# The opening pair of feed-forward tiles with gate and up alternating, and half of the last output projection's low halves by an adding DMA

## The chip, the cores and the metric

The kernel runs on one core of a Trainium2 chip. The metric is the time of one execution in microseconds (us), as the device counts it; three runs of the kernel before are at hand, and one more execution that the hardware profiler recorded.

## The reference, cut to what matters

One layer for 1088 tokens (1024 of a new stream, 64 of a running one), width 1024. Only the parts that the change touches are written out:

```
xn   = rmsnorm(x, norm_mix);  proj = xn @ w_in          # then three recurrent mixers on slices of proj
mix  = concat(oA, oB, oC)                               # 1088 x 1024
x    = x + mix @ w_out                                  # output projection, 1024 x 1024
xn2  = rmsnorm(x, norm_ffn)
hid  = silu(xn2 @ w_gate) * (xn2 @ w_up)                # feed-forward, 22 column tiles of 128
x    = x + hid @ w_down
y    = rmsnorm(x, norm_final)
```

## The kernel before, in words

**Tiles.** Tokens stand along the free axis in three groups of 384, 384 and 320 (groups 0, 1, 2); the width stands on the 128 partitions in 8 blocks. Each float32 operand is split in two: a high half that ScalarE (ACT) rounds to the matmul's format (`whi` for weights, line 117 or 1359), and a low half, the value less its high half. A product is then three products: high by high, high weight by low operand, low weight by high operand. A low half of a weight (`wlo`) is made in one of two ways: VectorE (DVE) subtracts (line 122 or 1360), or ACT writes the negated high half (line 119) and a DMA that GpSimd (POOL) issues adds the weight to it from memory (line 120). `weights(src, False)` chooses the first, `weights(src)` the second.

**Stages.** Up to about 440 us lie the input projection and the mixers. The program opens with `uproj(2)`, two column tiles of the input projection for group 2; `part` (line 1142) loads their weights in four halves. Then come the output projections, `outproj(0)`, `outproj(1)` and `outproj(2)`, 8 column tiles `dm` each; `outproj(2)` lies at 535.7 to 566.7 us. It begins with dm 0 and 1 together and takes the others one by one. `finish_dm` (line 187) adds the result to x (line 189) and sums squares (lines 211, 214). For the feed-forward's norm, `row_sums` sums squares over the partitions on TensorE (PE), `inv_rms` makes 1/rms by some fifteen short DVE instructions that end in two diagonal tiles `dg` (line 243), and `spread` lets PE broadcast them; the product of x with it is line 1295 for groups 0 and 1. `keep` (line 1285) has POOL store x in memory.

**Feed-forward.** The two halves of the width and groups 0 and 1 form 2x2 blocks, and `quad` (line 1390) makes a pair of column tiles with 7 block products instead of 8 (Winograd's form). Its operands are sums and differences of blocks of x: b11, d1, b22, s, d2, r2, r1, each of 4 blocks of 128x384, made by `operand` (line 1299): a sum `xs` (line 1305), ACT's cast (line 1307), DVE's low half (line 1308). `xs`, and the copies `t` and `u` in `quad`, are temporaries from one ring of four buffers (tag `xT`). Of the weights' sums, `raw` and `sm`, line 1396 is the DVE instruction. `quad` runs b11, b22, s, d1, d2, r2, r1; b11's result is copied by ACT to `t` (line 1407) before d1 is added into the same accumulator. One `product` is 12 matmuls. Group 2 is done plainly (`plain`, line 1382), with operands x2h and x2l that `x2prep` makes (DVE lines 264 and 266, ACT 265). For the first pair of tiles the order is: gate's quad, row sums and spread of group 2, `x2prep(2)`, up's quad, four plain products.

**What sets the order.** PE's order is the order in which the code calls `mm` (line 76 chains them). For the other engines a scheduler sets a fixed order when the program is built; `first()`, `soon()` and `high_priority` move an instruction forward in it. On the chip each engine then takes its instructions in that order, and waits at the first that is not ready.

## Time and profile before

| | us |
|---|---|
| three runs: median (lowest, highest) | 1385.15 (1383.03, 1387.94) |
| the profiled execution | 1381.88 |
| its span, first to last instruction | 1380.1 |
| PE busy in it | 1275.0 (92%) |
| DVE, ACT, POOL busy | 913.5, 660.0, 224.2 |
| output projection of group 2 to the end of the opening pair: from, to | 535.73, 648.52 |

The three runs differ by 4.9 us. The profiled execution is 3.3 us under their median; of its time 1.8 us lie outside the span. Busy time is the sum of an engine's instructions; a matmul's end is modelled. "Idle before" an instruction names what ended the idle time. The granted clock is 1.00 when TensorE runs at 2.4 GHz and 0.50 at 1.2 GHz.

### The profile page before, as it was taken

The numbers are of one execution on the slowest core, as the hardware profiler recorded it, in microseconds if no ns is written. First come the engines' busy times: TensorE is split into PE (matmuls) and PEld (weight loads), VectorE is DVE, ScalarE is ACT, GpSimd is POOL, SyncE is SP. The second block draws the span as 40 slices with busy tenths as digits, with TensorE's granted clock in tenths as the row PEclk, the third lists the DMA queues.
The fourth block names the chain that finished last, engine by engine and source line by source line (L and its number), as shares of the span: only waits on it lengthen the run. The fifth ranks groups of instructions, "written<-read, shape, count | busy, mean of one in ns | idle before, by whom it ended". The sixth has DMA issues, their size and how long they took to land.

```text
span 1380.1 us, 21112 instructions
## 1 busy us (share of the span) xinstructions
PE 1275.0 (92%) x7608; PEld 1214.8 (88%) x7608; DVE 913.5 (66%) x2206; ACT 660.0 (48%) x1288; POOL 224.2 (16%) x278
## 2 busy tenths in 40 slices
PE   7987998989988999759999999999999999999995
PEld 7876897878777889659999999999999999999985
DVE  9875798857766668976475437543763476346687
ACT  7766657768885444434243224412442243133463
POOL 2334354424342000020100000010001000100000
PEclk8997999999998899779999999999999999999997
DMA  9977687768884346303812551254125412631543
GB/s 285 287 148 180 138 172 147 172 142 177 164 188 107 104 162 212 116 15 96 164 39 71 117 96 38 77 107 92 55 71 110 80 54 77 107 78 62 184 141 111
DMA packets 94330, 170.60 MB, mean 124 GB/s; under 512 B 11425, under 2 KB 31473, under 8 KB 94225
## 3 DMA queue, kind: packets, MB, share of 16 engines
q1 hardware_dynamic: 70080, 108.26, 25.9%
q0 software_dynamic: 24144, 60.99, 25.0%
q8 instruction: 60, 0.98, 0.3%
q14 instruction: 46, 0.37, 0.1%
HBM read 134.76 MB, written 33.86 MB: 122 GB/s over the span
## 4 chain that ended last, share of the span: by engine, by line
PE 51%; DVE 3%; DMA 1%; issue 1%; ACT 0%; DVEq 0%; ACTq 0%
PE q L76 51%; DMA res<-st 1%; DVE wlo L122 1%; DVE u L1429 0%; DVE dg L243 0%; DVE x1r L1353 0%; DVE hl L1452 0%; DVE u L1430 0%; DVE sil L1450 0%; ACT whi L1359 0%; DVE sacc L214 0%; DVE sc L150 0%; DVE sc L149 0%; DVE sc L148 0%; DVE x1r L1480 0%
## 5 line engine op out<-in xcount | busy, mean ns | idle before, releaser
L117 ACT CAST whi<-raw 128x512 fp32r<-128x512 f32 (+1 forms) x232 | 139.5, 607 | 101.0 <-PE q L76 40.9
L76 PE MATMUL mm<-xh,whi 128*128 128x384 f32 (+1 forms) x480 | 168.8, 360 | 17.9 <-ACT whi L117 9.9
L76 PE MATMUL q<-hl,whi 128*128 128x384 f32 (+1 forms) x528 | 173.2, 332 | 2.7 <-DVE hl L1452 2.7
L76 PE MATMUL q<-hh,whi 128*128 128x384 f32 (+1 forms) x528 | 172.9, 331 | 2.1 <-ACT hh L1451 1.7
L76 PE MATMUL mm<-xl,whi 128*128 128x384 f32 (+1 forms) x480 | 159.6, 340 | 4.5 <-DVE xl L332 4.5
L120 POOL DMA_DIRECT2D wlo<-in_w_in_dram x112 | 99.4, 971 | 211.9 <-ACT wlo L119 180.1
L1482 DVE COPY st<-q 128x384 f32<-128x384 f32 x80 | 41.4, 524 | 134.3 <-PE q L76 118.5
L1493 POOL DMA_DIRECT2D res<-st x40 | 34.0, 851 | 585.9 <-DVE st L1482 499.7
L76 PEld LDWEIGHTS mm<-xh,whi 128*128 128x128 f32 x480 | 95.3, 200 | 25.5 <-ACT whi L117 10.5
L76 PE MATMUL q<-hh,wlo 128*128 128x384 f32 (+1 forms) x528 | 111.7, 330 | 0.0
L1359 ACT CAST whi<-raw 128x512 fp32r<-128x512 f32 x128 | 78.1, 621 | 67.4 <-PE q L76 53.9
L1360 DVE TENSOR_TENSOR wlo<-raw,whi 128x512 fp32r<-128x512 f32 x128 | 87.5, 685 | 29.6 <-ACT whi L1359 14.2
L76 PEld LDWEIGHTS q<-hl,whi 128*128 128x128 f32 x528 | 100.3, 190 | 4.9 <-DVE hl L1452 4.9
L76 PE MATMUL q<-x2l,whi 128*128 128x320 f32 x352 | 103.8, 309 | 0.0
L76 PE MATMUL q<-x2h,whi 128*128 128x320 f32 x352 | 103.8, 309 | 0.0
L76 PEld LDWEIGHTS q<-hh,whi 128*128 128x128 f32 x528 | 100.1, 190 | 4.0 <-ACT hh L1451 3.6
L122 DVE TENSOR_TENSOR wlo<-raw,whi 128x512 fp32r<-128x512 f32 (+1 forms) x120 | 80.1, 672 | 34.3 <-ACT whi L117 29.4
L76 PEld LDWEIGHTS mm<-xl,whi 128*128 128x128 f32 x480 | 94.8, 198 | 9.0 <-DVE xl L332 6.0
L76 PE MATMUL mm<-xh,wlo 128*128 128x384 f32 (+1 forms) x480 | 93.4, 335 | 6.1 <-DMA wlo<-in_w_in_dram 6.0
L1396 DVE TENSOR_TENSOR sm<-raw 128x512 f32<-128x512 f32 x66 | 45.6, 691 | 75.0 <-DMA raw<-in_w_up_dram 57.3
L76 PEld LDWEIGHTS q<-hh,wlo 128*128 128x128 f32 x528 | 91.6, 190 | 0.0
L76 PEld LDWEIGHTS mm<-xh,wlo 128*128 128x128 f32 x480 | 82.5, 193 | 8.9 <-DMA wlo<-in_w_in_dram 8.7
(467 smaller groups left out, 2930.8 us busy)
## 6 DMA issues: line engine op xcount, KB each, us to landing
raw<-in_w_in_dram SPq DMA_DIRECT2D x112, 256.0 KB, 4.3
wlo<-in_w_in_dram POOLq DMA_DIRECT2D x112, 256.0 KB, 6.0
res<-st POOLq DMA_DIRECT2D x40, 544.0 KB, 6.0
raw<-in_w_down_dram SPq DMA_DIRECT2D x56, 256.0 KB, 2.7
raw<-in_w_out_dram SPq DMA_DIRECT2D x48, 256.0 KB, 3.1
raw<-in_w_gate_dram SPq DMA_DIRECT2D x48, 256.0 KB, 2.9
raw<-in_w_up_dram SPq DMA_DIRECT2D x48, 256.0 KB, 3.0
xg<-in_x_dram SPq DMA_DIRECT2D x8, 512.0 KB, 6.3
```

The lines of the kernel that those rows point to most:

```text
L76: in_order(PE.matmul(out, lhsT, rhs, start=start, stop=stop, **kw).ins)
L117: ins = A.copy(hi[:, :n, :], raw[:, :n, :]).ins
L120: G.dma_start(lo[:, :n, :], src[:, h0:h0 + n, :], accum_op=OP.add)
L122: tt(lo[:, :n, :], raw[:, :n, :], hi[:, :n, :].bitcast(F32), op=OP.subtract)
L1359: A.copy(hi, src)
L1360: tt(lo, src, hi.bitcast(F32), op=OP.subtract)
L1396: tt(t_, a, b, op=op)
L1482: (A.copy if gi == 1 else V.tensor_copy)(st[:, t0:t0 + T], o[:, :T])
L1493: nc.gpsimd.dma_start(res[:, dm, :], st, accum_op=OP.add)
```

## The change

Nine edits, in the order of the diff.

1. `outproj(2)`'s sum of squares stands in another buffer (tag `hh` instead of `sil`).
2. In `outproj(2)` the weights of the odd dm (1, 3, 5, 7) get their low half by ACT and the adding DMA.
3. `uproj(2)`: both column tiles together, first high by high of both, then low operands, then low weights.
4. `inv_rms(0)` inside `soon()`.
5. The four weight halves of `uproj(2)` are loaded in the order m0, m1, m0, m1 instead of m0, m0, m1, m1.
6. The `xs` of operands s and d2 (4 each) on POOL instead of DVE; r2 and r1 were there already.
7. Row sums of group 1 behind dm 0 and 1, the spread straight behind them.
8. The opening pair: gate and up alternate through b11, d1, b22, s, d2, r2, r1; the weights' sums on POOL, in place; the weights of d1 and d2 loaded by themselves, with the low half by the adding DMA.
9. `x2prep(2)` behind the opening pair instead of between its two quads.

```diff
-        sacc = pool.tile([128, TMAX], F32, tag="sil" if gi == 2 else "sacc", name="sacc", bufs=2)
+        sacc = pool.tile([128, TMAX], F32, tag="hh" if gi == 2 else "sacc", name="sacc", bufs=4 if gi == 2 else 2)
...
-        first = [(weights(I["w_out"][dm], False), psd()) for dm in range(2)]
+        first = [(weights(I["w_out"][dm], gi == 2 and dm % 2 == 1), psd()) for dm in range(2)]
...
-                parts, o = weights(I["w_out"][dm], False), psd()
+                parts, o = weights(I["w_out"][dm], gi == 2 and dm % 2 == 1), psd()
...
+            if gi == 2:
+                for ks, js in ((range(4), (0,)), (range(4, 8), (0,)), (range(8), (1,)), (range(8), (2,))):
+                    for m in range(2):
+                        for j in js:
+                            for k in ks:
+                                mm(os[m][:, :T], parts[m][k][j == 2], acts(k)[j == 1],
+                                   start=(j == 0 and k == 0), stop=(j == 2 and k == 7))
...
-            diags = inv_rms(0, sc)
+            with soon():
+                diags = inv_rms(0, sc)
...
-            if k in (1, 5):
-                part(0, k - k % 4)
-        part(1, 0)
-        part(1, 4)
+            if k in (1, 3):
+                part(k // 2, 0)
+            if k in (5, 7):
+                part(k // 2 - 2, 4)
...
-        yield from operand("s", halves(bigtile("o_s")), b11, b22, OP.add)
+        yield from operand("s", halves(bigtile("o_s")), b11, b22, OP.add, G)
...
-        yield from operand("d2", halves(bigtile("o_d2")), b12, b22, OP.subtract)
+        yield from operand("d2", halves(bigtile("o_d2")), b12, b22, OP.subtract, G)
...
+        if i == 0:
+            with first():
+                diags = inv_rms(1, row_sums(1, [sums[1]], ps_t))
         if i == 1:
             with first():
-                diags = inv_rms(1, row_sums(1, [sums[1]], ps_t))
-        if i == 3:
-            spread(1, diags, ps_t, sums[1])
+                spread(1, diags, ps_t, sums[1])
...
+    def opening(src, post):
...
+        def summed(a, b, op):
+            with first():
+                x_, y_ = fresh(*a), fresh(*b)
+                G.tensor_tensor(x_, x_, y_, op=op)
+                return wsplit(x_)
...
+        product(oa, summed(a21, a22, OP.add), "b11")
+        with first():
+            A.copy(t_, oa[:, :TMAX])
+        yield
+        product(oa, weights_part(src[1], 4)[0], "d1", False)
...
+            both = [opening(I["w_gate"], gated), opening(I["w_up"], upped)]
+            for i in range(7):
+                if i == 2:
+                    with first():
+                        diags = inv_rms(2, row_sums(2, [sums[2]], ps_t))
+                if i == 3:
+                    with first():
+                        spread(2, diags, ps_t, sums[2])
+                    run2 = x2prep(2, p2, (bigtile("x2h2"), bigtile("x2l2")))
+                for g in both:
+                    next(g)
+            for _ in run2:
+                pass
```

Three places show how the built programs differ in order.

**PE in `outproj(2)`**, from the end of dm 0 and 1 (ml and mh are the low and high halves of mix) to the spread (`dg`). Before:

```order
L76 MATMUL q<-ones,sacc 128x1 x3
L76 MATMUL q<-mh_5732,whi 128x320
L76 MATMUL q<-ml_6031,whi 128x320
...
L76 MATMUL q<-mh_5732,wlo 128x320 x8
...
L76 MATMUL q<-mh_5732,wlo 128x320 x8
L76 MATMUL q<-dg,ones_r 128x384 x2
L76 MATMUL q<-mh_5732,whi 128x320
```

After:

```order
L76 MATMUL q<-mh_5732,wlo 128x320 x8
L76 MATMUL q<-ml_6031,whi 128x320 x16
L76 MATMUL q<-ones,sacc 128x1 x3
L76 MATMUL q<-dg,ones_r 128x384 x2
L76 MATMUL q<-mh_5732,whi 128x320
L76 MATMUL q<-ml_6031,whi 128x320
```

Between row sums and spread stood dm 2 and 3; now nothing does.

**ACT and POOL at the opening pair.** ACT's casts of the operands (`o_s`, `o_d`, `o_r` from the sums `xs`) and its copy `t` of b11's result, before:

```order
L1307 CAST o_s<-xs 128x384 x4
L1307 CAST o_d_6470<-xs 128x384 x2
L1359 CAST whi<-sm 128x512
L1307 CAST o_d_6470<-xs 128x384
L1307 CAST o_r_6487<-xs 128x384
L1307 CAST o_d_6470<-xs 128x384
L1307 CAST o_r_6487<-xs 128x384 x3
L1307 CAST o_r_6504<-xs 128x384 x4
L1407 COPY t<-q 128x384
```

ACT after (o_d_6478 is d2, o_r_6495 is r2, o_r_6512 is r1):

```order
L1317 CAST o_s<-xs 128x384
L1370 CAST whi<-raw 128x512
L1317 CAST o_s<-xs 128x384 x3
L1317 CAST o_d_6478<-xs 128x384 x4
L1317 CAST o_r_6495<-xs 128x384 x4
L1317 CAST o_r_6512<-xs 128x384 x3
L1422 COPY t<-q 128x384 x2
L1317 CAST o_r_6512<-xs 128x384
```

POOL after, behind the store of the last half of x (`res`); before, the store was followed by 8 `xs` and no weight sum (`raw`):

```order
L1295 DMA res<-x_2_6030 128x4x320
L1315 TENSOR_TENSOR xs<-x_0_5198,x_1_5646 128x384
L1414 TENSOR_TENSOR raw<-raw 128x512
L1315 TENSOR_TENSOR xs<-x_0_5198,x_1_5646 128x384 x3
L1315 TENSOR_TENSOR xs<-x_1_5646 128x384
L1414 TENSOR_TENSOR raw<-raw 128x512
L1315 TENSOR_TENSOR xs<-x_1_5646 128x384 x3
L1315 TENSOR_TENSOR xs<-x_0_5198,x_1_5646 128x384 x4
L1414 TENSOR_TENSOR raw<-raw 128x512
L1315 TENSOR_TENSOR xs<-x_0_5198,x_1_5646 128x384 x4
```

The copies `t` stood and stand behind casts whose sums POOL makes; POOL's part of them went from 8 sums to 16, with three weight sums between. On PE two products (b11 of gate and up) now stand ahead of d1; before, three did (b11, b22, s).

**DVE at the end of the opening pair** (u: the last sums of r1; xT and x2l: `x2prep`). Before:

```order
L243 TENSOR_TENSOR dg<-ident,sc 128x384
L219 MEMSET sc 128x9
L255 COPY sacc<-q 128x320
L264 SCALAR_TENSOR_TENSOR xT<-x_2_6029,cols,sacc 128x320 x2
L266 TENSOR_TENSOR x2l_6706<-xT,x2h_6705 128x320 x2
L264 SCALAR_TENSOR_TENSOR xT<-x_2_6029,cols,sacc 128x320 x2
L1360 TENSOR_TENSOR wlo<-raw,whi 128x512
```

After:

```order
L1445 TENSOR_TENSOR u<-q,t 128x384
L122 TENSOR_TENSOR wlo<-raw,whi 128x512
L1446 TENSOR_TENSOR u<-q,u 128x384
L264 SCALAR_TENSOR_TENSOR xT<-x_2_6029,cols,sacc 128x320
L1509 TENSOR_TENSOR sil<-u,sil 128x384
L264 SCALAR_TENSOR_TENSOR xT<-x_2_6029,cols,sacc 128x320
L266 TENSOR_TENSOR x2l_6705<-xT,x2h_6704 128x320
```

`x2prep` moved from the spread of group 2 to behind the last result of the opening pair, whose next PE work is the plain products that read x2h and x2l.

## Rows read from the trace of the kernel before

**Rows 1.** Windows: length, busy PE, PEld, DVE, ACT, POOL (instructions), clock, DMA share, GB/s.
```profile
20.00:40.00 20.00, 20.00 (x117) 20.00 (x117) 19.73 (x143) 16.53 (x35) 3.02 (x9) 0.96 0.99 311
700.00:1300.00 600.00, 597.50 (x3625) 594.33 (x3624) 331.14 (x582) 197.66 (x364) 29.88 (x35) 1.00 0.37 84
```

**Rows 2.** Waits of PE, 535 to 650 us: total, times, longest.
```profile
PE q L76 <- ACT t L1407: 14.2, 2, 12.1
```

**Rows 3.** Timeline of PE, `outproj(2)`: start, length, instruction, idle before and releaser.
```profile
551.72 0.44 PE L76 MATMUL q<-dg,ones_r 128*128 128x384 f32 x1 [1.01 <-DVE dg L243]
552.39 0.45 PE L76 MATMUL q<-dg,ones_r 128*128 128x384 f32 x1 [0.23 <-DVE dg L243]
...
558.54 1.33 PE L76 MATMUL q<-mh,wlo 128*128 128x320 f32 x8
...
562.06 1.33 PE L76 MATMUL q<-mh,wlo 128*128 128x320 f32 x8
```

**Rows 4.** Timeline of PE, the opening pair.
```profile
566.75 1.55 PE L76 MATMUL q<-o_b,whi 128*128 128x384 f32 x8
...
600.32 2.93 PE L76 MATMUL q<-o_d,whi 128*128 128x384 f32 x8 [12.14 <-ACT t L1407]
...
604.33 1.91 PE L76 MATMUL q<-o_d,whi 128*128 128x384 f32 x8
...
606.77 1.55 PE L76 MATMUL q<-o_r,whi 128*128 128x384 f32 x8
...
608.85 1.55 PE L76 MATMUL q<-o_r,whi 128*128 128x384 f32 x8
...
615.41 1.30 PE L76 MATMUL q<-dg,ones_r 128*128 128x320 f32 x2 [3.77 <-DVE dg L243]
616.51 2.59 PE L76 MATMUL q<-o_b,whi 128*128 128x384 f32 x8
...
633.76 0.85 PE L76 MATMUL q<-o_r,wlo 128*128 128x384 f32 x4
```

**Rows 5.** Timeline of DVE, chain of `inv_rms(1)`.
```profile
543.60 0.16 DVE L226 COPY sc<-q 128x3 f32<-128x3 f32 x1
...
548.22 0.69 DVE L122 TENSOR_TENSOR wlo<-raw,whi 128x512 fp32r<-128x512 f32 x1 [1.83 <-ACT whi L117]
...
551.78 0.56 DVE L243 TENSOR_TENSOR dg<-ident,sc 128x384 fp32r<-128x384 f32 x1
```

**Rows 6.** Timeline of DVE, chain of `inv_rms(2)`, then `x2prep(2)`.
```profile
611.68 0.16 DVE L226 COPY sc<-q 128x2 f32<-128x2 f32 x1
...
615.46 0.56 DVE L243 TENSOR_TENSOR dg<-ident,sc 128x384 fp32r<-128x384 f32 x1
...
617.27 1.02 DVE L264 SCALAR_TENSOR_TENSOR xT<-x,cols,sacc 128x320 f32<-128x320 f32 x2
618.35 0.95 DVE L266 TENSOR_TENSOR x2l<-xT,x2h 128x320 fp32r<-128x320 f32 x2
```

**Rows 7.** Timeline of DVE and of POOL, last x and the operands' sums.
```profile
576.91 0.48 DVE L189 TENSOR_TENSOR x<-q,xt 128x320 f32<-128x320 f32 x1
...
592.88 7.82 DVE L1308 TENSOR_TENSOR o_r<-xs,o_r 128x384 fp32r<-128x384 f32 x8
...
577.69 0.76 POOL L1285 DMA_DIRECT2D res<-x  x1 [22.81 <-DVE x L189]
...
593.04 6.31 POOL L1305 TENSOR_TENSOR xs<-x,x 128x384 f32<-128x384 f32 x5 [0.49 <-DVE o_d L1308]
```

**Rows 8.** Groups of POOL's sums by shape, whole span: count, busy us, mean ns.
```profile
L570 POOL TENSOR_TENSOR mix<-lr,gr 128x384 f32<-128x384 f32 x6 | 6.6, 1095 | 12.6 <-DVE gr L442 8.1 <-DVE sX L943 2.7 <-DVE lr L532 1.9
```

**Rows 9.** DMA issues of the page: KB each, median us to landing.
```profile
wlo<-in_w_in_dram POOLq DMA_DIRECT2D x112, 256.0 KB, 6.0
raw<-in_w_gate_dram SPq DMA_DIRECT2D x48, 256.0 KB, 2.9
```

**Rows 10.** Waits of PE, 0 to 26 us.
```profile
PE mm L76 <- DVE xl L332: 4.5, 3, 1.9
```

More of the change, by code (lines that the diff above doesn't have):

```diff
@@ L1388, in plain, with fresh, quad @@
             post(m, 2, o[:, :T])
-    def quad(src, m, post, with_g2):
+    def opening(src, post):
+        bufs = [0]
+        def fresh(dm, k):
+            bufs[0] += 1
+            pool, tag, n = ((wp, "raw", 3), (p2, "rw", 2))[bufs[0] % 2]
+            t_ = pool.tile([128, 4, 128], F32, tag=tag, name="raw", bufs=n)
+            nc.sync.dma_start(t_, src[dm][:, k:k + 4, :])
+            return t_
+        def summed(a, b, op):
[3 more added lines that the diff above has]
+                return wsplit(x_)
+        a11, a12, a21, a22 = (0, 0), (0, 4), (1, 0), (1, 4)
+        oa, ob, oc = ps_q(), ps_q(), ps_q()
+        t_ = temp("t")
+        product(oa, summed(a21, a22, OP.add), "b11")
[4 more added lines that the diff above has]
+        with first():
+            post(1, 0, oa[:, :TMAX])
+        yield
+        product(ob, summed(a11, a12, OP.add), "b22")
+        with first():
+            tt(t_, ob[:, :TMAX], t_, op=OP.add)
+        yield
+        product(oc, summed(a11, a22, OP.add), "s")
+        with first():
+            tt(t_, oc[:, :TMAX], t_, op=OP.subtract)
+        yield
+        product(ob, weights_part(src[0], 0)[0], "d2", False)
+        with first():
+            post(0, 1, ob[:, :TMAX])
+        yield
+        for x_, y_, name, acc, m, g in ((a12, a22, "r2", oa, 0, 0), (a21, a11, "r1", ob, 1, 1)):
+            o = ps_q()
+            product(o, summed(x_, y_, OP.subtract), name)
+            u = temp("u")
+            with first():
+                tt(u, o[:, :TMAX], t_, op=OP.add)
+                tt(u, acc[:, :TMAX], u, op=OP.add)
+                post(m, g, u)
+            yield
+    def quad(src, m, post):
         a11, a12, a21, a22 = raws(src[m], src[m + 1])
@@ L1455, in trunk @@
             sil = [p2.tile([128, NTOK], F32, tag="sil", name="sil", bufs=2) for _ in range(2)]
-            quad(I["w_gate"], m, gated, m > 0)
-            if m == 0:
-                with first():
-                    diags = inv_rms(2, row_sums(2, [sums[2]], ps_t))
-                spread(2, diags, ps_t, sums[2])
-                weave(x2prep(2, p2, (bigtile("x2h2"), bigtile("x2l2"))))
-            quad(I["w_up"], m, upped, m > 0)
-            if m == 0:
-                for src, post in ((I["w_gate"], gated), (I["w_up"], upped)):
-                    for i in range(2):
-                        plain(weights(src[i], False), post, i)
+            if m:
+                quad(I["w_gate"], m, gated)
+                quad(I["w_up"], m, upped)
+                continue
+            both = [opening(I["w_gate"], gated), opening(I["w_up"], upped)]
+            for i in range(7):
+                if i == 2:
+                    with first():
+                        diags = inv_rms(2, row_sums(2, [sums[2]], ps_t))
+                if i == 3:
+                    with first():
+                        spread(2, diags, ps_t, sums[2])
[4 more added lines that the diff above has]
+                pass
+            for src, post in ((I["w_gate"], gated), (I["w_up"], upped)):
+                for i in range(2):
+                    plain(weights(src[i], False), post, i)
         last = fi == len(ffg) - 1
```

13 lines of the change are left out of this document (7 added, 6 removed).

## The prediction

> **What bounds the kernel now.** I read the windows first. From 700 to 1300 us PE is busy 597.5 of 600 us at full clock [rows 1], so nothing there absorbs a delay: whatever the stretch before gives or takes stands in the final time, microsecond for microsecond. The stretch that the change rewrites, from the last output projection (about 536 us) to the end of the opening pair's plain products (648.5), is the opposite. PE's table of waits names its largest loss: 14.2 us behind ACT's copy `t`, 12.1 of them in one piece [rows 2], just before d1 at 600.32 [rows 4]. That name must be read with ACT's order: the copy needs only b11, done long before, but it stands behind the casts of r2 and r1, and those wait for the sums `xs` that POOL makes until 599.35 [rows 7]. So the true last link is POOL, not ACT. PE's timeline gives the unit prices: a dm of the output projection takes 3.52 us (558.54 to 562.06 [rows 3]), a product 2.08 (606.77 to 608.85 [rows 4]), a product that starts at half clock behind an idle stretch 4.0 (600.32 to 604.33 [rows 4]).
>
> I add up along PE, against the profiled execution (1381.88 us: span 1380.1 and 1.8 outside), and move the sum to the median of the three runs, 3.3 us higher, where results will be compared. Some 0.3%, or 4.2 us, is what a measurement of this kernel can tell from no change.
>
> **(a) The last output projection: about +6.6.** Before, the row sums stand 8 us ahead of the spread, with dm 2 and 3 between, and PE loses 1.24 us there [rows 3]. Afterwards the spread follows at once, so PE stands still for the whole chain of `inv_rms(1)`. That chain took 4.3 us undisturbed (611.68 to 616.02 [rows 6]) and 8.7 where a weight's low half that waited for its load stood in it (543.60 to 552.34 [rows 5]). I take 5.8, nearer the first row, as half of the low halves leave DVE; the difference is +4.6. Behind 3.77 us of idleness the next 8 matmuls took 2.59 instead of 1.55 [rows 4], so +1.0 for the clock. The low halves by DMA save DVE 8 subtractions, but PE did not wait for DVE here, so that is worth nothing on its path; it adds ACT's negation (like DVE's 0.69 for such a tile [rows 5]), POOL's issue (0.76 [rows 7]) and 6.0 to landing [rows 9], 7.4 us in a ring whose buffer comes free about two dm (7.04) earlier. Between 0 and 2.5 us of waits over four dm; I take 1.0.
>
> What the edit does gain comes later: before, the last x was added only at 576.91 [rows 7], 10 us behind its product, because DVE was behind. With 8 subtractions and 8 sums less DVE should keep up.
>
> **(b) From the end of dm 7 to d1: about -6.2.** Before: 566.75 to 600.32, 33.6 us [rows 4]. Afterwards I count POOL's queue from the end of dm 7, D. A low half and the last x on DVE (0.69 and 0.48), then the store's issue (0.76): D + 2.0. The `xs` of s and d2 now stand on POOL as well, so the copies `t` need 15 of POOL's 16 sums, and three weight sums lie between them. One sum: five in a row took 6.31, so 1.26 each, with DVE's low halves alternating at 0.98 instead of the 0.56 of a like instruction alone [rows 6, 7]: the two hold each other up. Where DVE does less, a POOL sum of this shape took 1.10 [rows 8]. I take 1.27, since the same pair alternates; the bounds are 1.10 and 1.66 (1.10 and 0.56, wholly one after the other). A weight sum is a third longer: 1.5, by the same rows 1.46 to 1.7. First sum: D + 3.3. The first weight sum waits for a load that is issued at D + 0.8 and lands 2.9 later [rows 9]: with issue, D + 4.0, done at 5.5. Four sums, 10.6; weight sum, 12.1; seven sums, 21.0; weight sum, 22.5; three sums, 26.3; a cast and the copy, about 1.0: d1 starts at D + 27.4. PE meanwhile has only the two b11 products, 4.2 us, so it stands still for 23 us. Before, POOL made 8 sums and DVE the rest, at the same time.
>
> The Trainium skill (GPSIMD Engine Reference, section 4.1, Engine selection) calls two-input elementwise work about twice as slow on GpSimd as on VectorE. With 0.56 that would be an estimated 1.12 per sum, less than the 1.26 that the row shows beside a busy DVE; (b) would be 2.3 us better and the time 1386.7. The sum goes by the row.
>
> **(c) From d1 to the end of r1: about -4.8.** Before: 600.32 to 634.61, 34.3 us, with 11 products, two waits (3.77 and 2.05) and two spells of half clock [rows 2, 4]. Afterwards 12 products: d1 of gate 4.0, d1 of up 2.44 (its start is slow too), row sums 0.55, both b22 4.2, then the spread, whose 4.3 us chain [rows 6] these two nearly cover: 1.2 of wait, since results of d1 stand in it on DVE, and 0.5 of work; then eight products, 16.6. Together 29.5. The weights of r2 and r1 pass through POOL behind its sums, but some 6 us or more ahead of their use.
>
> **(d) The plain products: about +8.4.** Before, `x2prep(2)` ran on DVE from 617.27 [rows 6], hidden beside the up quad. Afterwards it stands behind the last `u` of r1. Two of its eight blocks take 1.02 and 0.95 [rows 6], eight therefore 7.9; with two `u`, a `sil` and a low half ahead or between (0.5 each), the last x2l is ready 9.7 us after r1 ends. The first plain product would want it after 2.35 (16 of its 24 matmuls, two thirds of 3.52), so PE loses 7.4, and 1.0 more at half clock as in (a). If casts and low halves overlap better, the loss is 5.5; nothing else on PE can fill it, as its order is fixed.
>
> **(e) The start: 0.** PE waits 4.5 us for the low operands there [rows 10], and edits 3 and 5 put work into these waits; `uproj(2)` could end up to 2.7 us sooner. But from 20 to 40 us the DMA engines are 0.99 busy and PE has no gap [rows 1]; weights cannot come earlier, so I expect a lead to be waited away. Bounds: -2.7 to +1. Edits 1 and 4 change no wait that I can find: the buffer is not one that anybody waited for, and `inv_rms(0)` keeps nearly its place on DVE: nothing.
>
> **The sum:** 6.6 - 6.2 - 4.8 + 8.4 = +4.0. On the profile 1385.9, on the median **1389**. In words: the alternation shortens (c), DVE's relief shortens (b), and two things that were hidden, a spread and `x2prep`, come into the open for more.
>
> **Rivals.**
>
> *Not slower: the sums cost POOL less and the opened waits are short.* If POOL's sums run at 1.10 instead of 1.27, (b) falls by 2.6 and some 0.2 for the weight sums. For: the row of 1.10 [rows 8]. Against: DVE's low half follows each sum, as in the row of 1.26. This alone gives 1386.2; with the chain at 4.3, `x2prep`'s loss at 5.5 and a kept start lead, 1380.1. The point from which it decides: the sums would have to run below 1.0 each to bring (b) alone to no change.
>
> *Faster: the alternation does what its order suggests.* If the copies `t` went as soon as b11 is done, d1 and b22 would run beside POOL's sums, s would be ready at D + 11, r1 at D + 28, and r1 would end near D + 32 instead of D + 57: 1364 us. Against: ACT's order, fixed when the program is built, has 15 of the 16 casts ahead of the copies, and the same position cost 12.14 us before [rows 4].
>
> *Slower still: POOL and DVE wholly take turns.* At 1.66 a sum, (b) grows by 5.9: 1395. For: DVE also has weights' low halves in that stretch. Against: five sums in a row at 1.26. The place is d1's wait, and it decides from about 1.3 a sum.
>
> *The change does not do what it says:* the adding DMA relieves DVE, yet the last x still comes late because loads, not DVE, were late. Then (b) starts up to 5 us later: 1394. It counts with the case before.
>
> **How the numbers follow.** The forecast's case gets 0.50; it straddles the bound of 0.3% (1389.3), half of it slower, half no change. Not slower 0.26, of which 0.14 faster (under 1381) and 0.12 no change. Faster by the alternation 0.06. Slower still, with the case of late loads, 0.18. Faster 0.14 + 0.06 = 0.20; no change 0.25 + 0.12 = 0.37; slower 0.25 + 0.18 = 0.43. The range, 1379 to 1397, takes in all bounds of the forecast and of the first and third rival and leaves out the second and the joint ends.
>
> **What would show it.** (a) a wait of PE for `dg` of 4 to 8 us straight behind the row sums near 544. (b) the last x added on DVE within 2 us of its product; 16 sums of POOL at 1.2 to 1.35; one wait of PE for ACT's `t` near 23 us, d1 at half clock. (c) a wait for `dg` of about 1 us. (d) waits of PE for x2h and x2l, 6 to 8 us in all, right behind r1. It would be wrong if d1 starts within 20 us of dm 7's end, if the plain products run without waits, or if the time before 535 us moves by more than 3 us.

## The result: slower by 1.0%

The changed kernel takes 1400.5 us in the median (1393.76 to 1406.62), the kernel before 1386.65 (1383.03 to 1389.86) beside it: a ratio of 1.0102, with a 95% interval of 1.0073 to 1.0131. That is some 14 us more. Slower was the likeliest sign of the prediction, but 1400.5 lies above its 1389 and outside its range, which ended at 1397.

The profiled execution took 1398.88 us (span 1397.1), 17.0 more than the one of before. To see where, both traces are cut at the same four instructions: the first matmul of `outproj(2)`, the first of b11, the first of d1, and the first of the down projection, which follows the opening pair's plain products. "The stretch" is from the first of these to the last.

| | before | after | difference |
|---|---|---|---|
| start of `outproj(2)` | 535.73 | 538.76 | +3.0 |
| `outproj(2)` to b11 | 31.02 | 41.26 | +10.2 |
| b11 to d1 | 33.57 | 31.37 | -2.2 |
| d1 to the down projection | 48.20 | 55.02 | +6.8 |
| the stretch | 112.79 | 127.65 | +14.9 |
| down projection to the end of the span | 731.6 | 730.7 | -0.9 |

The stretch alone makes up the 14 us of the medians. The 3.0 us ahead of it are looked at below.

**The profile after.** First the windows; columns as in [rows 1]. The third line is the stretch's middle.

```profile
20.00:40.00 20.00, 18.15 (x90) 18.16 (x91) 15.56 (x121) 14.77 (x31) 1.98 (x5) 0.83 0.84 272
700.00:1300.00 600.00, 597.48 (x3628) 594.33 (x3628) 330.81 (x581) 197.58 (x364) 27.14 (x32) 1.00 0.36 79
...
550.00:600.00 50.00, 28.59 (x170) 27.40 (x170) 33.02 (x55) 21.46 (x42) 24.56 (x22) 0.81 0.69 187
```

The same 50 us in the kernel before:

```profile
550.00:600.00 50.00, 28.12 (x139) 24.01 (x138) 46.51 (x85) 21.19 (x43) 11.89 (x10) 0.74 0.27 90
```

From 700 us on nothing has changed against [rows 1]; PE is as full as it was, and gave nothing back. From 20 to 40 us PE, full before, now has gaps and a lower clock; that is the start, looked at in (e) below. In the stretch DVE is less busy (33.0 of 50 us against 46.5 before), POOL twice as busy (24.6 against 11.9), and the DMA engines went from 0.27 to 0.69. That last number was not in the prediction.

PE's waits from 535 to 660 us (total, times, longest), the four largest; [rows 2] has the largest of before, the copy `t`:

```profile
PE q L76 <- issue: 27.0, 1, 27.0
PE q L76 <- DVE dg L243: 7.6, 3, 6.1
PE q L76 <- ACT x2h L265: 3.6, 3, 2.7
PE q L76 <- DMA wlo<-in_w_out_dram: 3.1, 1, 3.1
```

"issue" means that the profile shows no releaser. It ends as the copy `t` does (rows below), and it goes when `t` gets a buffer of its own (e3), so it is the prediction's wait for `t`. PE's timeline shows the four in their places (start, length, instruction, idle before and releaser):

```profile
552.67 1.36 PE L76 MATMUL q<-dg,ones_r 128*128 128x384 f32 x2 [6.08 <-DVE dg L243]
553.83 0.47 PE L76 MATMUL q<-mh,whi 128*128 128x320 f32 x1
...
579.33 0.85 PE L76 MATMUL q<-mh,wlo 128*128 128x320 f32 x4 [3.08 <-DMA wlo<-in_w_out_dram]
580.02 1.55 PE L76 MATMUL q<-o_b,whi 128*128 128x384 f32 x8
...
611.38 2.90 PE L76 MATMUL q<-o_d,whi 128*128 128x384 f32 x8 [27.04 <-issue]
...
623.32 0.41 PE L76 MATMUL q<-dg,ones_r 128*128 128x320 f32 x1 [0.90 <-DVE dg L243]
...
624.58 2.08 PE L76 MATMUL q<-o_s,whi 128*128 128x384 f32 x8
...
645.66 0.48 PE L76 MATMUL q<-x2h,whi 128*128 128x320 f32 x1 [2.70 <-ACT x2h L265]
```

The wait of 3.08 is dm 7's: its low half comes by the adding DMA, and PE stops in the middle of its eight low-weight matmuls. POOL's and ACT's timelines show how it got late. L1414 is POOL's sum of two weight tiles, L1370 ACT's cast of such a sum, L119 its negation of dm 7's high half, L120 the adding DMA's issue:

```profile
571.06 2.54 POOL L1414 TENSOR_TENSOR raw<-raw 128x512 f32<-128x512 f32 x2 [2.92 <-DMA raw<-in_w_gate_dram]
573.82 0.86 POOL L120 DMA_DIRECT2D wlo<-in_w_out_dram  x1 [0.22 <-issue]
...
572.37 0.62 ACT L1370 CAST whi<-raw 128x512 fp32r<-128x512 f32 x1 [2.14 <-POOL raw L1414]
572.90 0.63 ACT L119 ACTIVATE wlo<-whi 128x512 fp32r<-128x512 f32 x1
```

A weight sum of the opening pair stands ahead in POOL's queue and waits 2.92 us for a gate load; ACT's cast of that sum waits for POOL; dm 7's negation stands behind the cast; the DMA is issued behind both and lands 5.5 us later. The opening pair reaches back into the output projection through two queues.

The other end, between dm 7's end (580.02) and d1 (611.38), by DVE, POOL and ACT. L1371 is the low half of a weight sum, L189 the last x, L1315 an operand's sum `xs`, L1295 the store, L1422 the copies `t`, L1317 the cast of an operand:

```profile
581.00 2.00 DVE L1371 TENSOR_TENSOR wlo<-raw,whi 128x512 fp32r<-128x512 f32 x1 [1.83 <-ACT whi L1370]
582.92 0.48 DVE L189 TENSOR_TENSOR x<-q,xt 128x320 f32<-128x320 f32 x1
...
583.71 0.80 POOL L1295 DMA_DIRECT2D res<-x  x1 [0.45 <-DVE x L189]
584.51 1.01 POOL L1315 TENSOR_TENSOR xs<-x,x 128x384 f32<-128x384 f32 x1
589.11 1.26 POOL L1414 TENSOR_TENSOR raw<-raw 128x512 f32<-128x512 f32 x1 [3.59 <-DMA raw<-in_w_gate_dram]
...
600.23 5.11 POOL L1315 TENSOR_TENSOR xs<-x,x 128x384 f32<-128x384 f32 x4
...
610.81 0.85 ACT L1422 COPY t<-q 128x384 f32<-128x384 f32 x2
611.66 0.52 ACT L1317 CAST o_r<-xs 128x384 fp32r<-128x384 f32 x1
```

This is the queue that the prediction counted, with the sums at 1.28 each in a run of four (four of the sixteen, with no low half beside them, took 1.0), and one wait of 3.59 us in it that is much longer than was counted.

### The profile page after: what moved, and what is told of

It reads as the page before. It is cut to its first block, busy times and chain, and to the rows that moved or that the text cites. A ratio compares the mean times of both kernels' runs of the same rounds, so it can differ in the third digit from the quotient of the medians.

```text
span 1397.1 us, 21167 instructions
## 1 busy us (share of the span) xinstructions
PE 1274.7 (91%) x7608; PEld 1215.9 (87%) x7608; DVE 904.4 (65%) x2176; ACT 666.2 (48%) x1300; POOL 258.6 (19%) x308
## 4 chain that ended last, share of the span: by engine, by line
PE 64%; DVE 15%; issue 7%; DMA 6%; ACT 4%; POOL 4%; SPq 0%; DVEq 0%; ACTq 0%; POOLq 0%
PE q L76 52%; PE mm L76 8%; PE mx L76 4%; DMA wlo<-in_w_in_dram 2%; DMA raw<-in_w_out_dram 1%; DVE wlo L122 1%; POOL wlo L120 1%; POOL xs L1315 1%; DMA raw<-in_w_gate_dram 1%; ACT whi L117 1%; ACT L138 1%; DMA raw<-in_w_in_dram 1%; DMA res<-st 1%; DVE mix L1069 1%; ACT wlo L119 1%
## 5 line engine op out<-in xcount | busy, mean ns | idle before, releaser
L120 POOL DMA_DIRECT2D wlo<-in_w_in_dram x112 | 99.9, 981 | 216.3 <-ACT wlo L119 185.2
L76 PEld LDWEIGHTS mm<-xh,whi 128*128 128x128 f32 x480 | 94.8, 199 | 28.8 <-ACT whi L117 13.7
L1371 DVE TENSOR_TENSOR wlo<-raw,whi 128x512 fp32r<-128x512 f32 x130 | 91.6, 705 | 41.9 <-ACT whi L1370 23.7
L1370 ACT CAST whi<-raw 128x512 fp32r<-128x512 f32 x130 | 79.3, 621 | 80.0 <-PE q L76 56.4
L122 DVE TENSOR_TENSOR wlo<-raw,whi 128x512 fp32r<-128x512 f32 (+1 forms) x112 | 74.8, 670 | 39.4 <-ACT whi L117 27.1
L76 PE MATMUL q<-o_d,whi 128*128 128x384 f32 x352 | 69.7, 340 | 28.4 <-issue 27.0
```

The costliest lines, as they stand in the source:

```text
L76: in_order(PE.matmul(out, lhsT, rhs, start=start, stop=stop, **kw).ins)
L120: G.dma_start(lo[:, :n, :], src[:, h0:h0 + n, :], accum_op=OP.add)
L122: tt(lo[:, :n, :], raw[:, :n, :], hi[:, :n, :].bitcast(F32), op=OP.subtract)
L1370: A.copy(hi, src)
L1371: tt(lo, src, hi.bitcast(F32), op=OP.subtract)
```

## The experiments

The table holds all of them, cut at the same instructions; times in us, from each kernel's trace. "b11 to d1" holds two products in the alternating order and three (b11, b22, s) in the order of before. The last column is the ratio to the kernel before with its 95% interval.

| kernel | `outproj(2)` to b11 | b11 to d1 | d1 to down | stretch | ratio |
|---|---|---|---|---|---|
| before; again | 31.0; 31.2 | 33.6; 33.8 | 48.2; 48.2 | 112.8; 113.2 | 1 |
| after | 41.3 | 31.4 | 55.0 | 127.7 | 1.0102 [1.0073, 1.0131] |
| e1 edits 3, 5 undone | 41.6 | 30.9 | 55.1 | 127.6 | 1.0112 [1.0082, 1.0143] |
| e7 edits 3, 4, 5 undone | 42.6 | 31.6 | 56.3 | 130.5 | 1.0102 [1.0069, 1.0136] |
| e2 edit 7 undone | 36.8 | 29.4 | 53.6 | 119.9 | 1.0087 [1.0057, 1.0117] |
| e6 edits 8, 9 undone | 38.7 | 32.3 | 47.7 | 118.7 | 1.0042 [1.0017, 1.0066] |
| e9 edit 2 undone | 38.2 | 33.8 | 53.2 | 125.1 | 1.0098 [1.0064, 1.0132] |
| e5 edit 6 undone | 42.3 | 29.0 | 56.3 | 127.6 | 1.0107 [1.0074, 1.0140] |
| e12 weight sums on DVE | 37.9 | 31.6 | 52.2 | 121.7 | 1.0081 [1.0054, 1.0108] |
| e3 `t` in a ring of its own | 42.1 | 5.7 | 76.2 | 123.9 | 1.0104 [1.0067, 1.0141] |
| e4 e3, `x2prep` earlier | 42.4 | 5.7 | 66.5 | 114.6 | 1.0024 [1.0004, 1.0045] |
| e8 reordered | 31.2 | 11.7 | 61.2 | 104.0 | 0.9939 [0.9909, 0.9968] |
| e10 reordered, `x2prep` first | 30.9 | 7.5 | 67.8 | 106.2 | 0.9962 [0.9941, 0.9983] |

By the intervals of the last column only e6, e4, e8 and e10 differ from the changed kernel. What the others show, they show in one trace each. The stretch of e7 has the changed kernel's code and took 2.9 us longer, so a difference of some 3 us in the stretch proves little by itself; it is read together with the wait that came or went.

### The start: e1, e7 and the kernel before again

e1 puts edits 3 and 5 back, the order of `uproj(2)` and of its loads; e7 also edit 4, `soon()`.

```diff
-            if k in (1, 3):
-                part(k // 2, 0)
-            if k in (5, 7):
-                part(k // 2 - 2, 4)
+            if k in (1, 5):
+                part(0, k - k % 4)
+        part(1, 0)
+        part(1, 4)
```

> The changed kernel with edits 3 and 5 undone: uproj(2) one column tile after the other, its four weight halves loaded in the old order. Theory A (the two edits cost the start: PE waited 2.7 us for a low half by DMA at 21.9 us and then ran on at half clock to 29 us): uproj(2) ends at 24.7 us as before, the last output projection starts at 535 to 536 us instead of 538.8, and the time falls by about 3 us, to 1397.5. Rival B (the 3 us come from another edit or from the order of the mixers): the start gets back its old rows, but the last output projection still starts at 538 to 539 and the time stays at 1400.

> The changed kernel with edits 3, 4 and 5 undone: the start as before and inv_rms(0) without soon(). With 3 and 5 alone undone the start was that of before, yet the output projection of group 2 began at 539.3, and the lag grew by 3.7 us between 380 and 440 us, where inv_rms(0) stands. Theory A (edit 4 costs this): it begins at 535 to 537 us and the time falls by 3 to 4 us, to 1397. Rival B (the mixers' stretch varies from one build or one execution to the next by this much, whatever edit 4 does): it begins at 538 to 540 again and the time falls by less than 2 us.

> The kernel before, unchanged, for a second trace. Theory A (the start of the last output projection varies from one execution to the next through the mixers' stretch): it begins between 534 and 541 us, away from 535.7, while the stretch from there to the down projection takes 112.8 us again, within 1 us. Rival B (the traces of the changed kernels begin it at 537 to 542 because of edits): it begins at 535.7, within 0.5 us.

The start of `outproj(2)` moved from 538.76 to 539.34 (e1) and 541.66 (e7): later, not sooner, and the times did not fall, as rival B had it; e7 came later than either of its theories said. The kernel before, traced again, came there at 535.19, nearly as its rival B had it, its stretch the same to 0.4 us. But e8 and e10 below, whose code ahead of 535 us is that of the kernel before, came there at 534.25 and 539.71. So nothing ties the 3.0 us to the start's edits. Whether the change makes the mixers later at all, by way of the order that the scheduler gives them, stays open: kernels with the same code there differ by 5 us.

### The spread: e2

Edit 7 undone: the row sums behind dm 2, the spread two dm later, as before.

```diff
-        if i == 0:
+        if i == 1:
             with first():
                 diags = inv_rms(1, row_sums(1, [sums[1]], ps_t))
-        if i == 1:
-            with first():
-                spread(1, diags, ps_t, sums[1])
+        if i == 3:
+            spread(1, diags, ps_t, sums[1])
```

> The changed kernel with edit 7 undone: row sums of group 1 behind dm 1, the spread behind dm 3. Theory A: PE's wait for dg near 547 to 553 us falls from 6.1 us to 1 or 2, the spell at half clock behind it goes, dm 7 ends some 6 us sooner and the time falls by 5 to 6 us, to 1395. Rival B (weights arrive no sooner, so a shorter wait here is waited away at dm 7's low halves and at the first weight sums): dm 7's wait for its DMA grows from 3.1 to over 5 us or d1 starts at the same place, and the time falls by less than 2 us.

In the trace the stretch fell by 7.8 us, and the 6.08 us wait for `dg` went with the half clock behind it: theory A's mechanism. The times show some 2 us of it (1.0087 against 1.0102, with intervals that overlap), where theory A had 5 to 6; the raw median of 1394.89 was measured beside a kernel before that was itself faster, at 1383.45. Why the time gained less than the stretch stays open. And the stand for the spread had been covering something. PE's timeline of e2, the matmuls that waited for a low half by DMA:

```profile
554.55 0.85 PE L76 MATMUL q<-mh,wlo 128*128 128x320 f32 x4 [0.91 <-DMA wlo<-in_w_out_dram]
555.90 0.85 PE L76 MATMUL q<-mh,wlo 128*128 128x320 f32 x4 [0.51 <-DMA wlo<-in_w_out_dram]
...
564.38 0.86 PE L76 MATMUL q<-mh,wlo 128*128 128x320 f32 x4 [0.83 <-DMA wlo<-in_w_out_dram]
...
575.42 1.44 PE L76 MATMUL q<-mh,wlo 128*128 128x320 f32 x4 [3.73 <-DMA wlo<-in_w_out_dram]
```

Where PE doesn't stand still for the spread, the adding DMA is late for dm 3 and 5 as well: 6.0 us in all, a part of rival B.

### The low halves, the weight sums and dm 7: e9, e12, e6

e9 undoes edit 2 (`weights(I["w_out"][dm], False)` for every dm): all low halves of the output projection on DVE. e12 leaves edit 2 and has DVE make the weight sums, so that POOL's queue holds none:

```diff
-                G.tensor_tensor(x_, x_, y_, op=op)
+                tt(x_, x_, y_, op=op)
                 return wsplit(x_)
```

e6 undoes edits 8 and 9: `quad` and its order of before, weight sums on DVE, `x2prep(2)` between the quads; edits 1 to 7 stay.

> The changed kernel with edit 2 undone: all low halves of the last output projection on DVE. In the changed kernel PE waited 3.1 us for dm 7's second low half: ACT's negation for it stood behind ACT's cast of the opening pair's first weight sum, that behind POOL's sum, and that behind a load. Theory A (this chain and the added DMA traffic are what edit 2 costs): the wait at dm 7 goes, and from the first matmul of the output projection to the first of the down projection it takes 122 to 125 us instead of 127.7, the time falls by 3 to 5. Rival B (DVE falls behind again without edit 2, so the last x and with it POOL's queue come as much later): d1 starts 3 or more us later after dm 7's end, and the stretch stays within 1.5 us of 127.7.

> The changed kernel with one edit: the sums of two weight tiles in the staging buffers, which GpSimd makes, are made by VectorE. Everything else is as in the changed kernel; GpSimd keeps the sixteen operand sums, the adding stores and its transfers. The question is what makes the stretch from the last output projection tile's end to the down projection's first matmul 31.4 us long, where 27.4 were forecast. Theory A: the weight sums stand ahead of the operand sums in GpSimd's queue and wait there for weight loads (3.6 us in one place) and take 1.3 us each. With them gone GpSimd works only on operand sums, so this stretch shortens by 5 to 8 us, to 23 to 26, and the whole stretch from the last output projection's first matmul to the down projection's first matmul is 120 to 123 us instead of 127.7. Rival B: the loads themselves pace everything, since ScalarE's weight casts stand ahead of the operand casts and wait for the same loads, and VectorE, which now waits for them as well, falls behind with the x tiles: the stretch stays within 2 us of 31.4 or grows, and the whole stays at 126 to 130 us.

> The changed kernel with edits 8 and 9 undone: the opening pair is the quad of the kernel before, gate after up, x2prep between; edits 1 to 7 stay. Theory A (the pair's new order costs 9.4 us in the plain products and gains 5 ahead of and in the products, the rest of the 17 us lies ahead of it): dm 7 ends near 580 us as in the changed kernel, the plain products run without waits, and the time lies at 1392 to 1396. Rival B (the alternation itself pays, and only edits 1 to 7 cost): the time stays at 1400 or rises.

In each of the three dm 7's wait is gone, and `outproj(2)` is 3.1, 3.4 and 2.6 us shorter. It takes both: a low half by DMA and a weight sum ahead of it in POOL's and ACT's queues. In e6 the low halves of four dm came by the adding DMA too, and PE waited for none. What edit 2 was to bring is there as well: without it (e9) the last x is done 6.8 us behind dm 7's end instead of 3.4, and d1 comes 2.4 us later behind b11. So e9 lies between its theories: the stretch is 2.5 us shorter, and by its time it can't be told from the changed kernel.

From b11 to d1, e12 went against its theory A: 31.6 us, not 23 to 26, with no weight sum left on POOL. Its DVE, POOL, ACT and PE:

```profile
587.38 0.69 DVE L1414 TENSOR_TENSOR raw<-raw 128x512 f32<-128x512 f32 x1 [4.51 <-DMA raw<-in_w_gate_dram]
...
588.62 2.65 POOL L1315 TENSOR_TENSOR xs<-x 128x384 f32<-128x384 f32 x2 [2.04 <-DVE o_s L1318]
...
605.63 0.51 ACT L1317 CAST o_r<-xs 128x384 fp32r<-128x384 f32 x1 [0.75 <-POOL xs L1315]
606.05 0.85 ACT L1422 COPY t<-q 128x384 f32<-128x384 f32 x2
...
606.62 2.90 PE L76 MATMUL q<-o_d,whi 128*128 128x384 f32 x8 [27.27 <-issue]
```

DVE now waits 4.51 us for the load in POOL's place; the low halves behind it free no buffer of the `xs` ring, and POOL stands still for 2.04 and 1.10 us. The load's lateness moved from one queue to the other. Two more things moved with it. DVE, which now makes the weight sums, is done with the last x only 5.9 us behind dm 7's end instead of 3.4. And the copies `t` stand behind all 16 casts, where 15 stand ahead of them in the changed kernel, so that they wait for one sum more, 1.3 us. Together these ate what the weight sums had taken, so e12 does not show what the weight sums alone cost. The stretch was 5.9 us shorter all the same, as theory A's second number had it, for another reason: 3.4 at dm 7, 2.8 behind d1, most of it since the products of s ran at full clock.

e6 says what edits 8 and 9 cost together: 8.9 of the 14.9 us. Edits 1 to 7 alone cost 5.9.

### The operand sums: e5

Edit 6 undone: the sums of s and d2 on DVE again.

```diff
-        yield from operand("s", halves(bigtile("o_s")), b11, b22, OP.add, G)
+        yield from operand("s", halves(bigtile("o_s")), b11, b22, OP.add)
-        yield from operand("d2", halves(bigtile("o_d2")), b12, b22, OP.subtract, G)
+        yield from operand("d2", halves(bigtile("o_d2")), b12, b22, OP.subtract)
```

> The changed kernel with edit 6 undone: the sums of operands s and d2 on DVE, so that POOL makes 8 of the 16 and the weights' sums. Theory A (POOL's queue sets d1, at 1.27 us per sum): eight sums fewer take 10 us out of it, DVE needs 4 to 5 us for them beside its low halves, d1 starts 4 to 8 us nearer to the end of dm 7 than 31.4 us, and the time falls to 1392 to 1396. Rival B (POOL's 3.4 and 3.6 us waits for weight loads and the late last x set it): the start of d1 moves by less than 2 us.

The prediction's price for these eight sums was 8 times 1.27, some 10 us of POOL's queue. Taking them away shortened b11 to d1 by 2.4 us, between rival B (under 2) and theory A (4 to 8), and the stretch by nothing: the rest was lost again ahead of b11 and behind d1. POOL's timeline of e5, its three weight sums behind the store, and ACT's at the copies `t`:

```profile
588.73 1.25 POOL L1414 TENSOR_TENSOR raw<-raw 128x512 f32<-128x512 f32 x1 [5.16 <-DMA raw<-in_w_gate_dram]
590.96 1.52 POOL L1414 TENSOR_TENSOR raw<-raw 128x512 f32<-128x512 f32 x1 [0.98 <-DMA raw<-in_w_up_dram]
595.63 2.14 POOL L1414 TENSOR_TENSOR raw<-raw 128x512 f32<-128x512 f32 x1 [3.15 <-DMA raw<-in_w_gate_dram]
...
607.61 0.51 ACT L1317 CAST o_r<-xs 128x384 fp32r<-128x384 f32 x1 [0.76 <-POOL xs L1315]
608.03 0.85 ACT L1422 COPY t<-q 128x384 f32<-128x384 f32 x2
```

With nothing to do in between, POOL waits 9.3 us for loads instead of 3.6: of the 10 us that the sums had taken, 5.7 went there. A weight sum wants two tiles; their buffers come free when the sum before has been cast and its low half made; only then can the next load start, which took 3.8 us in the median from 560 to 600 us of after, and 5.9 once. This circle runs beside the sums, and comes out where they are taken away: the waits are rival B's. Some 1.3 us more were no matter of loads: as in e12, the copies `t` stand behind all 16 casts here.

### The copies `t`: e3 and e4

The copy of b11's result stands behind the casts because `t` is the next user of the ring of four temporaries. e3 gives it another ring:

```diff
-        t_ = temp("t")
+        t_ = p2.tile([128, TMAX], F32, tag="hl", name="t", bufs=4)
```

> The changed kernel, with the copies t of the opening pair in free buffers of another ring (tag hl) instead of the ring of the sums xs; nothing else is edited. Theory A (the 27 us in front of d1 are there because the copies wait in ACT's order for ring buffers that the last sums on POOL use): d1 starts within 2 us of b11's end, PE then waits in pieces for s, d2, r2 and r1 as POOL delivers them, r1 ends 18 to 24 us sooner, and the time falls to 1376 to 1383, below the kernel before. Rival B (POOL's sums bound the pair wherever the copies stand): the wait only moves to s and behind, and the time falls by less than 8 us.

This is the rival that the prediction gave 0.06, made true: d1 straight behind b11. It gave 3.7 us in the stretch and nothing that the times show. PE's timeline of e3, then DVE's, of the chain that the second row waited for:

```profile
593.88 2.93 PE L76 MATMUL q<-o_d,whi 128*128 128x384 f32 x8 [3.95 <-ACT t L1422]
...
619.06 0.63 PE L76 MATMUL q<-dg,ones_r 128*128 128x320 f32 x1 [14.13 <-DVE dg L243]
...
603.73 0.14 DVE L226 COPY sc<-q 128x2 f32<-128x2 f32 x1
...
607.13 2.66 DVE L148 TENSOR_TENSOR sc<-sc 128x3 f32<-128x3 f32 x1
...
620.54 0.55 DVE L243 TENSOR_TENSOR dg<-ident,sc 128x384 fp32r<-128x384 f32 x1
```

The 27 us became 4 + 14 us of waits and spells of half clock. The row sums of group 2 now come while the operand sums are still being made, and the chain of `inv_rms(2)`, 4.3 us undisturbed [rows 6], takes 17.4 between the low halves of d2, r2 and r1. PE's order has the spread ahead of s, and so stands still. Rival B had said that the wait would only move.

e4 adds one thing: `x2prep(2)` is emitted behind the fourth step, right after the spread, instead of behind the pair.

```diff
                 for g in both:
                     next(g)
-            for _ in run2:
-                pass
+                if i == 3:
+                    for _ in run2:
+                        pass
```

> As e3_t_own, and x2prep(2) emitted behind the spread of group 2, ahead of the opening pair's s products, instead of behind the pair (edit 9 undone in its effect). Theory A (the plain products wait because x2prep stands on DVE behind the last result of r1, at 643 to 656 us): the waits of PE for x2h and x2l (4.2 us) and the half clock there go, the first plain product takes 3.5 to 4 us instead of 12.6, and the time lies 7 to 9 us below e3. Rival B (x2prep's 16 instructions only shift DVE's other work, the low halves and results of the pair): PE waits as long ahead of r2 and r1 and the difference to e3 is under 3 us.

The stretch fell by 9.4 us against e3, as theory A had it, and the plain products run without a wait behind r1, whose last matmuls start at 639.36:

```profile
640.05 0.31 PE L76 MATMUL q<-x2h,whi 128*128 128x320 f32 x1
640.20 0.30 PE L76 MATMUL q<-x2l,whi 128*128 128x320 f32 x1
```

The time fell with it, from 1.0104 to 1.0024. So edit 9 cost its term (d), here measured by itself, and with `t` free it can be had back.

### A version that beats both: e8 and e10

e8 keeps the alternating pair, its weight sums on POOL and the adding DMA for d1 and d2; undoes edits 2 to 7; gives `t` the ring of e3; and moves the second chain one step up, the row sums ahead of d1 and the spread ahead of b22, with `x2prep` behind that step:

```diff
             for i in range(7):
-                if i == 2:
+                if i == 1:
                     with first():
                         diags = inv_rms(2, row_sums(2, [sums[2]], ps_t))
-                if i == 3:
+                if i == 2:
                     with first():
                         spread(2, diags, ps_t, sums[2])
...
+                if i == 2:
+                    for _ in run2:
+                        pass
```

> The alternating pair without what held it up: edits 2 to 7 undone, copies t in the other ring, row sums of group 2 behind the two b11, their spread behind the two d1, x2prep behind that. Theory A (the alternation is sound and only DVE's and ACT's orders and the DMA traffic spoilt it): d1 starts within 2 us of b11, PE's waits between dm 7 and the end of the pair fall from 40 us to under 20, the plain products run without a wait, and the time lies at 1368 to 1378, below the kernel before. Rival B (the sums of the operands and the loads bound the pair in any order): the waits only move, and the time is 1383 to 1390.

1377.28 us in the median, against 1383.18 for the kernel before beside it, a ratio of 0.9939: faster than the kernel before by 0.6% and, by the two ratios, than the changed one by 1.6%. The traced execution was the fastest of its ten (1369.31); the stretch, 8.8 us shorter than before, is nearer to what the ratio says. The time is theory A's, at its upper end. The waits are not quite: behind dm 7 they come to 21 us, and the plain products still wait. PE's timeline has four waits of more than 1.5 us left:

```profile
575.90 1.29 PE L76 MATMUL q<-ones,sacc 128*128 128x1 f32 x6 [6.13 <-issue]
...
589.55 0.63 PE L76 MATMUL q<-dg,ones_r 128*128 128x320 f32 x1 [6.33 <-DVE dg L243]
...
620.13 0.61 PE L76 MATMUL q<-x2h,whi 128*128 128x320 f32 x1 [6.59 <-ACT x2h L265]
...
626.30 0.41 PE L76 MATMUL q<-x2l,whi 128*128 128x320 f32 x1 [1.83 <-DVE x2l L266]
```

e10 goes for the last two: row sums and spread one step later, `x2prep` pulled forward with `first()`, and `u` out of the shared ring too.

```diff
-            u = temp("u")
+            u = p2.tile([128, 4, 128], F32, tag="sm", name="u", bufs=1)
...
+                if i == 3:
+                    with first():
+                        for _ in run2:
+                            pass
```

> As e8_reordered, with three differences: row sums of group 2 behind d1 and the spread behind b22, as in the changed kernel; x2prep inside first(); the results u in a buffer of their own, so that x2prep does not wait for them. In e8 PE still waited 6.1 us for the row sums, 6.3 for dg and 8.4 for x2h and x2l. Theory A (these are waits of order, not of work): the 8.4 us and most of the 12.4 go, the stretch from the output projection to the down projection takes 88 to 95 us instead of e8's 104, and the time falls to 1362 to 1370. Rival B (DVE's and POOL's work in the stretch is the bound): the waits reappear ahead of s, r2 or r1, and the time stays within 3 us of e8's 1377.

The waits for x2h and x2l went and came back elsewhere, in the same view:

```profile
598.44 0.64 PE L76 MATMUL q<-dg,ones_r 128*128 128x320 f32 x1 [8.36 <-DVE dg L243]
...
625.28 0.69 PE L76 MATMUL q<-o_r,whi 128*128 128x384 f32 x1 [9.03 <-DVE o_r L1309]
```

With `x2prep` ahead, DVE's low halves of r1 are late, in its first product. Moving DVE's work changed which product waits, as rival B had it; whether another order would leave no wait, no run shows.

## Why the prediction missed

The sign, the places of all four waits and most prices of instructions were right. The sum was +4.0 for the stretch and came to +14.9; each of four terms fell short, the same way. The two steps that failed most are the price of a load in (b), a term that came 4.0 us short, and the low halves by DMA in (a), 2.1 of the 3.6 us that it came short.

**(a), +6.6 forecast, +10.2 measured.** The wait for `dg` was put at 5.8 and is 6.08; the half clock behind it at 1.0 and is some 1.4 in dm 2 (twelve matmuls start 0.27 us apart instead of 0.15) and 0.5 in the spread. The miss is the low halves by DMA: 1.0 forecast with an upper bound of 2.5, 3.08 measured. The failed step is "7.4 us in a ring whose buffer comes free about two dm (7.04) earlier": it adds up the operation's own parts and puts nothing ahead of them. What stood ahead, shown by e9 and e12, was a weight sum on POOL that waits for its load, and ACT's cast behind it. The instructions of the order to come were listed for the opening pair, not for how far back they reach.

**(b), -6.2 forecast, -2.2 measured.** The sums were priced at 1.27 and took 1.28 where a low half stood behind each; the three weight sums at 1.5 took 1.26 to 1.57; d1 stood behind `t`, and `t` behind 15 casts, as forecast, and ran at half clock. Counted from the first weight sum's end, d1 came 21.0 us later; 21.9 were forecast. All of the miss lies ahead of that point. The last x was done at dm 7's end + 3.4 and not + 1.2 (the prediction's own sign was within 2 us), since DVE's low half before it waited for the cast of a late weight sum and then took 2.00 instead of 0.68 beside POOL's next. And the failed step, "a load that is issued at D + 0.8 and lands 2.9 later", became a load issued at 583.03, D + 3.0 (its buffer came free only with that low half), which let POOL go on at 589.11, 6.1 later. The 2.9 is a whole program's median [rows 9]; in this stretch the DMA engines were at 0.69 instead of 0.27, and at 0.98 from 585 to 590 us. That the load was late for this reason is read from these shares; no run shows it by itself. The prediction read prices of instructions from the stretch, but the price of a load from everywhere.

A fix of the term by itself would have been too simple, as e5 shows. When half of the sums were taken away, the circle of loads, which the term didn't count, came out and took more than half of what they had cost. So the chain that came out nearly in its length, 21.0 us for 21.9, was only one of two. No run took the sums and the loads away together, so how long this part would be without either stays open.

**(c), -4.8 forecast, -2.7 measured.** The spread waited 0.90 and 0.59 where 1.2 was said. Not counted was the clock behind it: the first s product took from 624.58 to 627.73 and the second to 630.31, 5.73 instead of the 4.16 of two products, +1.6.

**(d), +8.4 forecast, +9.5 measured.** From r1's end (642.96) to the down projection it is 23.45 us, before 13.91. The sum was close and its split was not: not one wait of 7.4 and 1.0 of clock, but waits of 4.2 in five pieces, and between them matmuls at half clock, because the blocks of x2 come one at a time. So the closeness of the sum is in part luck. e4 shows that the cause is `x2prep`'s place.

**(e), 0 forecast.** In the trace of after the wait for low operands [rows 10] is gone from the list of PE's waits to 26 us and one of 2.7 for low weights stands there. There was no lead to keep: behind that wait PE ran on at a lower clock (0.69 from 25 to 30 us, 1.00 before) and came later to the same matmul of the next tile, the second row here; the last row is before's.

```profile
21.85 3.57 PE L76 MATMUL mm<-xh,wlo 128*128 128x320 f32 x12 [2.73 <-DMA wlo<-in_w_in_dram]
...
29.30 1.55 PE L76 MATMUL mm<-xh,wlo 128*128 128x384 f32 x8
...
27.38 1.55 PE L76 MATMUL mm<-xh,wlo 128*128 128x384 f32 x8
```

These 1.9 us lie outside the term's bounds of -2.7 to +1. e1 has them back at that point (27.48; the other traces with the old start lie between 27.2 and 28.8) and not at `outproj(2)`, so they did not reach the stretch. One of the prediction's own conditions, that the time before 535 us should not move by over 3 us, was just broken (3.03). e1 and e7, where undoing the start's edits gave nothing back, speak against these edits as the cause.

**The rivals.** The sums did not run at 1.10 beside DVE's low halves, so "not slower" lost its ground. "Faster by the alternation" was set aside for the right reason, and e3 shows that it would not have held even with `t` free: it left out the spread's chain and `x2prep`. POOL and DVE did not take turns at 1.66. The last rival came nearest: "loads, not DVE" were late. It was priced at 5 us in one place and counted with the case before; in fact it acted in three, at dm 7, at the last x and in POOL's queue. The range left out the joint ends, and this one cause moved several terms to their ends together.

The Trainium skill (GPSIMD Engine Reference, section 4.1, Engine selection), with its factor of about two, had given an estimated 1.12 per sum and with it 1386.7 us. A sum with no low half beside it took 0.99 at 598.02 us of this trace against DVE's 0.55, which agrees with the factor; beside a busy DVE it was 1.28. The row was the better price, and neither decided the result.

## What to carry to other kernels

When work is moved to another engine's queue, list everything in that queue which can wait for a load, and who stands behind it, back into the stage before; an instruction that waits for memory costs the whole queue its wait. Price a load by the DMA share that the stretch will have after the change, and look for the circle of load, sum, cast, buffer and next load beside the chain of the engine. A spread or a norm's chain that PE's fixed order puts right behind its row sums is paid in full, and once more in clock; with two dm between them, as e2 puts back, the 6.08 us wait and the half clock were gone. And where an experiment moves one instruction, read the built order again before its number: in e5 and e12 the copies `t` moved too.

## What the runs showed of the hardware

- **A chain of tiny VectorE instructions beside GpSimd's sums.** In e3 the norm's chain took 17.4 us where 4.3 were seen alone. Besides the low halves between them, single instructions on 128x3 elements grew from 0.17 to 0.96, 1.19 and 2.66 us. The one of 2.66 ran from 607.13 to 609.79, over two sums of GpSimd in a row, which ended at 609.75. The Trainium skill (SBUF — State Buffer, section "SBUF: two separate sides") says that a VectorE instruction with two inputs in SBUF and a GpSimd one that reads SBUF take turns on a shared port pair, which the one that starts first holds for its whole instruction. This row agrees as to the waiting; by the trace VectorE's instruction had started 0.13 us ahead of the first sum and waited out both all the same.
- **Such turns do not add up in full for large sums.** With a low half of VectorE's behind each, a sum took 1.28 us: less than the 0.99 and 0.55 that the two took alone, put together. The low half took 1.10 there.
- **A load of 256 KB** that took 2.9 us in the median of the whole program [rows 9] let its user go on after 6.1 us in a stretch where the DMA engines were at 0.69.
- **Kernels with the same code ahead of 535 us** reached it at times up to 5 us apart (e8 and e10), while the stretch of one kernel came out the same to 0.4 us (before, twice). Stretches cut at the same instructions tell more than spans, but not everything: e7's stretch, with the code of after, came out 2.9 us longer.
